# Split projection weights kept in DRAM: stored by the second token block, loaded as two halves by the third and fourth

## The chip, the core and the metric

The kernel runs on one core of one Trainium2 chip. The metric is the device time of one execution in microseconds (us). Engines are named as the profile names them: PE (TensorE matmul), PEld (its weight load), DVE (VectorE), ACT (ScalarE), POOL (GpSimd) and SP (SyncE). SP here does little but issue DMAs; ACT issues a few as well.

## The reference

One decoder block over 2048 tokens of width 1024 in float32. The part that matters here is the combined projection of the mixer:

```python
h = modulate(rms_norm(x, g_pre_mix[l]), shift_m, scale_m)
proj = h @ w_in[l]
q_a, k_a, v_a, q_m, k_m, v_m, o_m, i_m, f_m, g_a, g_m = jnp.split(proj, split_points, axis=-1)
...
y_a = sliding_window_attention(rope(q_a), rope(k_a), v_a, sinks)
h_m = mlstm_chunkwise(q_m, k_m, v_m, i_pre, f_pre)
merged = sigmoid(g_a) * (y_a @ w_branch_attn) + sigmoid(g_m) * (y_m @ w_branch_mlstm)
x = x + gate_m * rms_norm(merged @ w_out, g_post_mix)
```

After this comes a SwiGLU feed-forward with the same kind of norm and gate. `q_a` has 512 columns, `k_a` and `v_a` 128 each, `v_m` 512; the two pre-gates `i_m` and `f_m` have 4 each.

## The kernel before

**Numbers as two halves.** PE multiplies in a format (F32R) that holds fewer bits than float32. So every operand is split in two: `hi` is the value rounded to that format, `lo` the rest. A product is then three matmuls: hi x hi, hi x lo, lo x hi (`mm3`, L283). For weights the split is made by `split` (L255): ACT casts to `whi` (L267, or L264 for q, whose heads are put in pairs, one 512-column slice at a time), DVE subtracts to get `wlo` (L268 or L265).

**Token blocks.** The 2048 tokens go through in four blocks of 512, two to a superblock. Blocks are numbered 0 to 3 in the code; the text calls them one to four. For each block three projections have the tokens on the output's partitions: q (512 columns), kv (264 columns: keys, values, pre-gates) and vm (512 columns, the mLSTM values). Each is a `token_group` (L318): the 1024 input features are eight slices of 128, taken two at a time, which makes four pieces. A piece is 4 token tiles x 2 slices x 3 terms = 24 matmuls into four accumulators (`acc`), evacuated by ACT after the last piece (L778, L805, L829). The first block is written out by hand and takes q and kv in its own way; in it only vm is a `token_group` with loads and splits like the others. The second block takes kv, q, vm; the third q, kv, vm; the fourth kv, q, vm. Every block loads the same columns of `w_in` and splits them again.

**Loads and buffers.** A q or vm load (L298) brings four slices, 1 MB, which serve two pieces; kv comes as one tile for all four pieces (two DMAs, L784 and L785). Loads go into one of two `raw` buffers. A split takes a pair of `split` buffers, of which there are four, so two pairs. A raw buffer is free when its last split has read it; a split pair is free when PE has done the piece.

**What sets the order.** `run2` (L352) goes through all pieces. Before a piece it makes the splits of this piece and the next (`ahead=2`), and issues loads while fewer than two raw tiles are loaded and not yet split. Side work runs in streams that are woven between the matmuls by a count of expected PE time (`now`, with the delays L_...): attention, mLSTM chunks, rotary work on q and k, the next block's norm and transposes. `attend` (L1016) ends the q and k streams and starts attention for the block; `finish` advances the streams with no matmuls of the projection between. The instructions of each engine are then put in a fixed order by the tile scheduler, which runs its own timeline. Each engine, and each DMA-issuing queue, works strictly through that order.

**DRAM in between.** Attention's operands are stored to `at_d` (L771, L798, L816, L818) from tiles called `tx`, of which there are nine, and loaded again (L908, L910); vm goes to `vm_d` (L830). All of these are issued by SP, but for some attention loads and stores by ACT.

Of the kernel before, what the change touches and what calls it, by code (L numbers as in the profile page):

```python
# [10 lines left out]
F32 = mybir.dt.float32  # L11
F32R = mybir.dt.float32r
# [7 lines left out]
P = 128  # L20
S = 2048
D = 1024
KD = D // P
# [31 lines left out]
C_Q, C_K, C_QM, C_KM, C_VM, C_OM, C_IF, C_GA, C_GM = 0, 512, 768, 1280, 1792, 2304, 2816, 2824, 3848  # L55
# [18 lines left out]
def decoder_block(ctx: ExitStack, tc: tile.TileContext, a: dict, out: bass.AP, dbg=None):  # L74
    nc = tc.nc
# [21 lines left out]
    w_in = a["w_in"][0]  # L97
# [6 lines left out]
    wpool = ctx.enter_context(tc.tile_pool(name="wpool", bufs=2))  # L104
# [19 lines left out]
    def tx(shape, dtype=F32):  # L124
        return tpool.tile(shape, dtype, tag="tx", name=nm("tx"), bufs=9)
# [64 lines left out]
    for i in range(HD // 2):  # L190
        f = np.float32(10000.0) ** np.float32(np.float32(-2.0) * np.float32(i) / np.float32(HD))
# [53 lines left out]
    RAWC = KD * 264  # L245
# [6 lines left out]
    def split_tile(name):  # L252
        return wpool.tile([P, 1024], F32R, tag="split", name=nm(name), bufs=4)

    def split(src, shape, pair_heads=False, eng=V):  # L255
        n = int(np.prod(shape))
        hi, lo = split_tile("whi"), split_tile("wlo")
        hv = hi[:, :n].rearrange("p (k c) -> p k c", k=shape[0])
        lv = lo[:, :n].rearrange("p (k c) -> p k c", k=shape[0])
        if pair_heads:  # L260
            for k in range(shape[0]):
                sv = src[:, k, :].rearrange("p (g j d) -> p g j d", g=HKV, d=HD)
                hk, lk = (v[:, k, :].rearrange("p (j g d) -> p g j d", g=HKV, d=HD) for v in (hv, lv))
                A.copy(hk, sv)  # L264
                V.tensor_tensor(lk, sv, hk.bitcast(F32), op=ALU.subtract)  # L265
        else:
            A.copy(hv, src)  # L267
            V.tensor_tensor(lv, src, hv.bitcast(F32), op=ALU.subtract)  # L268
        return hv, lv
# [10 lines left out]
    def piece(raw, view, shape, mms, pair_heads=False):  # L280
        return Part(raw, lambda: split(view(raw.tile), shape, pair_heads), mms)

    def mm3(ps, l, r, first, last):  # L283
        mm(ps, l[0], r[0], first, False)
        mm(ps, l[0], r[1], False, False)
        mm(ps, l[1], r[0], False, last)
# [8 lines left out]
    def raw_rows(w, k0, nk, c0):  # L295
        def load():
            t = raw_tile([nk, 512])
            nc.sync.dma_start(t, w[k0 * P:(k0 + nk) * P, c0:c0 + 512].rearrange("(k p) c -> p k c", p=P))  # L298
            return t
        return Raw(load)  # L300
# [14 lines left out]
            for j in range(2):  # L315
                yield feature_tile(raw, lambda t, j=j: t[:, :, j * P:(j + 1) * P], k, i0 + j, rhs, evac)

    def token_group(srcs, nk, n, lhs, evac, pair_heads=False, stagger=1):  # L318

        acc = []  # L320
        srcs = list(srcs)
        held = []

        def make(si, k0, kc):
            def mms(wt):
                if not acc:
                    acc.extend(acc_tile() for _ in range(NT))
                held.append((wt, k0, kc))
                if len(srcs) - stagger <= si < len(srcs) - 1:
                    return  # L330
                for t in range(NT):
                    for w_, k0_, kc_ in held:
                        for j in range(kc_):
                            kk = k0_ + j
                            mm3(acc[t][:, :n], lhs(kk, t), (w_[0][:, j, :], w_[1][:, j, :]), kk == 0, kk == nk - 1)
                            yield
                    if si == len(srcs) - 1:
                        evac(t, acc[t])
                held.clear()
            return mms  # L340

        for si, (raw, view, k0, kc) in enumerate(srcs):
            yield piece(raw, view, [kc, n], make(si, k0, kc), pair_heads)

    def srcs_rows(w, nk, c0):
        for k0 in range(0, nk, 4):
            kn = min(4, nk - k0)
            raw = raw_rows(w, k0, kn, c0)
            for j in range(0, kn, 2):
                yield raw, (lambda t, j=j: t[:, j:j + 2, :]), k0 + j, 2  # L350
# [350 lines left out]
    def ld(shape, dtype=F32):  # L701
        t = kvp.tile([P, 512], dtype, tag="ld", name=nm("ld"), bufs=4)
        return t.rearrange("p (k c) -> p k c", k=shape[0])
# [24 lines left out]
    om_d = [tc.dram_tile([P, MH, TB], F32, name=f"om_d{i}") for i in range(NBLK)]  # L728
    g_d = [tc.dram_tile([P, 2, KD, TB], F32, name=f"g_d{i}") for i in range(NBLK)]
    y_d = [tc.dram_tile([P, 4, 4, TB], F32, name=f"y_d{i}") for i in range(NBLK)]  # L730
    LOGC = math.log(MD ** -0.5)
    LOG2 = math.log(2.0)

    def superblock(sb):
# [3 lines left out]
        def lhs_h(b):  # L738
            def lhs(kk, t):
                return tuple(p_[:, kk % 4, t * P:(t + 1) * P] for p_ in HC[f"{kk // 4 + 1}{b % 2 + 1}"])  # L740
            return lhs
# [19 lines left out]
        def q_stream(b, t, yz):  # L761
            yield L_ROPE
            y, z = yz
            pt = mix_tile()
            for j in range(GQ):
                transpose(pt[:, j * P:(j + 1) * P], y[:, j * P:(j + 1) * P])
            hi, lo = z.bitcast(F32R), y.bitcast(F32R)
            A.activation(hi, pt, AF.Copy, scale=HD ** -0.5)
            V.scalar_tensor_tensor(lo, pt, HD ** -0.5, hi.bitcast(F32), op0=ALU.mult, op1=ALU.subtract)
            for i, q in enumerate((hi, lo)):  # L770
                nc.sync.dma_start(at_d[b * NT + t][:, i * 512:(i + 1) * 512], q.bitcast(F32))  # L771
# [28 lines left out]
        def evac_kv(b):  # L800
            before = [v_last]

            def evac(t, ps):
                raw = ld([1, 512])[:, 0, :] if b == 0 else tx([P, 392])
                A.copy(raw[:, :264], ps[:, :264])  # L805
                v, dv = raw[:, 128:256], raw[:, 264:392]
                n = b * NT + t
                y = rope(raw, HKV, b, t)
                for i in range(2):
                    A.copy(gt[:, t, 32 * i:32 * i + 4], raw[:, 256 + 4 * i:260 + 4 * i])  # L810
                V.tensor_tensor(dv, v, before[0], op=ALU.subtract)
                before[0] = v
                if t == NT - 1:
                    A.copy(v_last, v)
                    before[0] = v_last
                nc.sync.dma_start(at_d[n][:, AT_V + P:], dv)  # L816
                if n + 1 < S // P:
                    nc.sync.dma_start(at_d[n + 1][:, AT_V:AT_V + P], v)  # L818
                R["qk"].append(spawn(k_stream(n, y)))
            return evac  # L820

        def q_kv(b):
            raw_kv = Raw(load_kv)
            return token_group(srcs_rows(w_in, KD, C_Q), KD, 512, lhs_h(b), evac_q(b), pair_heads=True), token_group([(raw_kv, (lambda r, j=j: r[:, j:j + 2, :]), j, 2) for j in range(0, KD, 2)], KD, 264, lhs_h(b), evac_kv(b))

        def vm(b):
            def evac(t, ps):
                v = tx([P, 512])
                A.copy(v, ps)  # L829
                nc.sync.dma_start(vm_d[b][:, t, :], v)  # L830
            yield from token_group(srcs_rows(w_in, KD, C_VM), KD, 512, lhs_h(b), evac)


        def gates(b):
# [56 lines left out]
            mpv = mp.rearrange("p h (k c) -> p k c h", k=2)  # L891
            V.scalar_tensor_tensor(ex[:, 0], cl[:, :, 0, :], LOGC - LOG2, mpv[:, 1], op0=ALU.add, op1=ALU.add)
            V.tensor_copy(ex[:, 1], cl[:, :, 2, :])
            V.tensor_tensor(ex[:, 2], mpv[:, 0], mpv[:, 1], op=ALU.add)
            A.activation(ex, ex, AF.Exp)
            V.tensor_scalar(cl[:, :, 0, :], cl[:, :, 0, :], LOGC - 2.0 * LOG2, None, op0=ALU.add)
            V.tensor_scalar(mp[:, :, 0:4], mp[:, :, 0:4], -LOG2, None, op0=ALU.add)
# [98 lines left out]
        ready = [0]  # L996
# [358 lines left out]
        for i, (kind, p) in enumerate(pairs):  # L1355
            parts = list(in_pair(kind, p))
            if sb == 0 and i == 4:
                yield lambda: R.update(ada_m=[spawn(ada_stream([(2, "gate")], 6000.0))])
            if i == 0:
                yield from parts[:3]  # L1360
                yield lambda: finish([hps["t"]])
                parts = parts[3:]
            if i + 1 == len(pairs):
# [3 lines left out]
                parts = parts[2:]  # L1367
# [843 lines left out]
```

## Time and profile before

| | us |
|---|---|
| median of 3 runs | 2673.64 (2673.51 to 2677.0) |
| the profiled execution's own time | 2673.95 |
| its span, first to last instruction | 2672.2 |
| PE busy | 2620.8 (98%) |
| DVE busy | 1964.5 (74%) |
| ACT busy | 1304.4 (49%) |
| DMA moved | 511.84 MB, mean 192 GB/s |
| granted clock of PE, mean | 0.995 |

The span is what the profiler sees of the program; the execution's own time is 1.75 us more. The profile gives for each group of instructions its busy time, the mean of one in ns, and the idle time of its engine before it with what ended that time. A row of the waits says who waited for whom: us in total, how often, the longest. In a row of busy times by stretch the columns are the stretch, its length, the busy time of PE, PEld, DVE, ACT and POOL with the instructions' count, the granted clock, the share of the 16 DMA engines that was busy, and what they moved.

In this execution the second block's kv, q and vm pieces run from about 98 to 176 us, the third block's from about 692 to 757, the fourth block's from about 757 to 850.

### The profile page before, as it was taken

The page shows a single profiled execution, that of the slowest core. Times are in us where ns is not written, and L with a number is a line of the kernel's source. Part 1 is how long each engine was busy: PE and PEld are TensorE (multiplying, and loading weights), DVE is VectorE, ACT ScalarE, POOL GpSimd, SP SyncE. Part 2 cuts the span into 40 slices and gives each one's busy share as a digit, 9 for nine tenths or more (in the row PEclk, how much of TensorE's full clock was granted, in tenths as well). Part 3 has the DMA queues.
Part 4 walks back from the last instruction along what each step waited for, and adds up shares of the span by engine and source line. Part 5 has one row for each costly group of instructions (what it writes and reads, how often), then busy time and mean ns, then how long its engine had stood idle before and what let it go on. Part 6 is the DMA issues. An engine that isn't in the chain of part 4 may idle for free.

```text
span 2672.2 us, 36050 instructions
## 1 busy us (share of the span) xinstructions
PE 2620.8 (98%) x12546; PEld 2145.7 (80%) x12546; DVE 1964.5 (74%) x3790; ACT 1304.4 (49%) x2563; POOL 136.3 (5%) x181
## 2 busy tenths in 40 slices
PE   8999999999998999999999999999999999999998
PEld 6877788888876778888878888888778888888886
DVE  6877887768786988875777777775776767676466
ACT  6666544445764654454654443335554333333444
POOL 0000002101100000110000000000000000000000
PEclk9999999999999999999999999999999999999999
DMA  7664455987576645687675555446675323234566
GB/s 269 202 222 138 140 192 182 306 296 256 186 232 197 194 133 165 191 269 294 205 260 173 175 173 177 145 150 215 213 252 180 110 99 105 101 111 138 191 203 221
DMA packets 353062, 511.84 MB, mean 192 GB/s; under 512 B 24544, under 2 KB 213084, under 8 KB 347632
## 3 DMA queue, kind: packets, MB, share of 16 engines
q1 hardware_dynamic: 334664, 493.76, 55.6%
q10 hardware_dynamic: 18216, 15.79, 2.0%
q8 instruction: 99, 1.62, 0.2%
q14 instruction: 83, 0.68, 0.1%
HBM read 357.06 MB, written 144.02 MB: 188 GB/s over the span
## 4 chain that ended last, share of the span: by engine, by line
PE 84%; DVE 6%; DMA 5%; ACT 2%; issue 2%; POOL 0%; SPq 0%; ACTq 0%; DVEq 0%; POOLq 0%
PE acc L212 59%; PE mix L212 22%; PE mix L217 2%; DVE hl L1701 1%; DMA big<-big 1%; PE acc L90 1%; PE mix L90 1%; ACT hl L1700 1%; DMA raw<-as_d 1%; DMA big<-in_x_dram 1%; DMA at<-at_d 1%; DMA raw<-ws_d 1%; DMA at_d<-tx 1%; ACT tm L958 0%; DMA raw<-in_w_ffn_down_dram 0%
## 5 line engine op out<-in xcount | busy, mean ns | idle before, releaser
L212 PE MATMUL acc<-big,hl 128*128 128x512 f32 x3936 | 936.7, 392 | 3.6 <-ACT tx L829 1.5
L212 PEld LDWEIGHTS acc<-big,hl 128*128 128x128 f32 x3936 | 732.2, 188 | 163.5 <-issue 5.5
L1700 ACT CAST hl<-raw 128x512 fp32r<-128x512 f32 x732 | 440.6, 622 | 488.2 <-PE acc L212 219.5
L1701 DVE TENSOR_TENSOR hl<-raw,hl 128x512 fp32r<-128x512 f32 x732 | 496.4, 695 | 198.5 <-ACT hl L1700 195.9
L212 PE MATMUL acc<-whi,big 128*128 128x512 f32 (+1 forms) x1152 | 344.6, 378 | 3.7 <-ACT tx L829 1.6
L212 PE MATMUL mix<-big,hl 128*128 128x512 f32 x1056 | 263.0, 390 | 1.6 <-ACT hl L1700 0.9
L212 PEld LDWEIGHTS acc<-whi,big 128*128 128x128 f32 x1152 | 212.1, 190 | 43.3 <-ACT tx L805 2.4
L212 PE MATMUL acc<-hl,hl 128*128 128x512 f32 x1008 | 237.3, 393 | 5.9 <-DVE hl L1701 3.4
L212 PEld LDWEIGHTS mix<-big,hl 128*128 128x128 f32 x1056 | 197.8, 188 | 44.3 <-DVE hl L1701 1.8
L212 PEld LDWEIGHTS acc<-hl,hl 128*128 128x128 f32 x1008 | 186.9, 188 | 51.6 <-DVE hl L1701 8.8
L212 PE MATMUL acc<-wlo,big 128*128 128x512 f32 (+1 forms) x576 | 217.6, 379 | 3.6 <-DVE wlo L268 3.3
L212 PE MATMUL mix<-hl,hl 128*128 128x512 f32 x792 | 182.9, 391 | 1.2 <-DVE ms L456 0.4
L212 PEld LDWEIGHTS mix<-hl,hl 128*128 128x128 f32 x792 | 147.8, 188 | 35.5 <-DVE hl L1701 3.3
L212 PE MATMUL acc<-big,whi 128*128 128x512 f32 x512 | 157.3, 393 | 0.0
L268 DVE TENSOR_TENSOR wlo<-raw,whi 128x1024 fp32r<-128x1024 f32 (+1 forms) x92 | 106.9, 1163 | 67.2 <-ACT whi L267 61.6
L267 ACT CAST whi<-raw 128x1024 fp32r<-128x1024 f32 (+1 forms) x92 | 91.9, 1000 | 117.3 <-PE acc L212 111.2
L212 PEld LDWEIGHTS acc<-wlo,big 128*128 128x128 f32 x576 | 109.9, 191 | 24.1 <-DVE wlo L268 4.8
L458 POOL TENSOR_TENSOR rs<-ms,halves 128x1 f32<-128x1 f32 (+1 forms) x56 | 41.6, 754 | 1640.2 <-DVE ms L456 1592.3
L212 PE MATMUL mix<-hcT4h,hl 128*128 128x512 f32 x352 | 115.6, 389 | 0.7 <-ACT hl L1700 0.7
L212 PE MATMUL acc<-hcT2h,hl 128*128 128x512 f32 x352 | 115.5, 389 | 0.0
L212 PEld LDWEIGHTS acc<-big,whi 128*128 128x128 f32 x512 | 95.3, 188 | 19.3
L212 PE MATMUL acc<-big,wlo 128*128 128x512 f32 x256 | 97.5, 392 | 0.0
(377 smaller groups left out, 3542.0 us busy)
## 6 DMA issues: line engine op xcount, KB each, us to landing
raw<-in_w_in_dram SPq DMA_DIRECT2D x46, 1024.0 KB, 5.2
as_d<-w SPq DMA_DIRECT2D x154, 256.0 KB, 2.0
raw<-as_d SPq DMA_DIRECT2D x70, 512.0 KB, 3.7
raw<-in_w_ffn_gate_dram SPq DMA_DIRECT2D x22, 1024.0 KB, 5.7
raw<-in_w_ffn_up_dram SPq DMA_DIRECT2D x22, 1024.0 KB, 5.9
raw<-ws_d SPq DMA_DIRECT2D x40, 512.0 KB, 4.5
tx<-in_w_ada_dram SPq DMA_DIRECT2D x64, 256.0 KB, 5.2
g_d<-tx SPq DMA_DIRECT2D x64, 256.0 KB, 2.5
```

Of the source, the lines that this page charges most:

```text
L90: self.last = tc.keep_in_program_order(f(*p, **k)).ins
L212: T.matmul(o, lhsT=lhsT, rhs=rhs, start=start, stop=stop, skip_group_check=resumed)
L217: T.transpose(o, i, ident[:k, :k])
L267: A.copy(hv, src)
L268: V.tensor_tensor(lv, src, hv.bitcast(F32), op=ALU.subtract)
L458: G.tensor_tensor(r[:, :n], ms[:, :n], nhalf[:, :n], op=ALU.pow)
L1700: A.copy(v(hi), src)
L1701: V.tensor_tensor(v(lo), src, v(hi).bitcast(F32), op=ALU.subtract)
```

## The change

The second block, after each split of a q, kv or vm piece, also stores both halves to DRAM arrays `W_D` (24 stores: 512 KB each for q and vm, 264 KB for kv). The third and fourth block no longer load `w_in` for these three and no longer split: they load the halves. Even q and vm pieces go as one 1 MB load of both halves into a raw buffer, odd ones as two 512 KB loads straight into a split pair; kv goes as two loads of 1056 KB, each of two pieces with both halves, into raw buffers. Each such load is a `Raw` of its own, its `Part` has nothing to prepare (`ready` only shapes the views), and the matmuls read the raw tile or split pair directly. So a raw buffer then stays in use up to the piece's last matmul. The matmuls themselves, their count and their operands' values are the same.

```diff
+    def kept_weights(name):
+        n = 528 if name == "kv" else 1024
+        for j0 in range(0, 4, 2):
+            for j in ((j0,) if name == "kv" else (j0, j0 + 1)):
+                def load(j=j):
+                    src = W_D[name]
+                    if name != "kv" and j % 2:
+                        parts = [split_tile(x) for x in ("whi", "wlo")]
+                        for i in range(2):
+                            nc.sync.dma_start(parts[i].bitcast(F32), src[:, j, i, :])
+                        return [parts]
+                    m = 2 if name == "kv" else 1
+                    t = wpool.tile([P, RAWC], F32R, tag="raw", name=nm("raw"))
+                    v = t[:, :m * 2 * n].rearrange("p (m i c) -> p m i c", m=m, i=2)
+                    nc.sync.dma_start(v.bitcast(F32), src[:, j:j + m, :, :])
+                    return [[v[:, q, i, :] for i in range(2)] for q in range(m)]
+                raw = Raw(load)
+                for q in range(2 if name == "kv" else 1):
+                    yield raw, q, 2 * (j + q), 2
...
         for si, (raw, view, k0, kc) in enumerate(srcs):
-            yield piece(raw, view, [kc, n], make(si, k0, kc), pair_heads)
+            if kept:
+                def ready(raw=raw, q=view):
+                    return tuple(v.rearrange("p (k c) -> p k c", k=2) for v in raw.tile[q])
+                yield Part(raw, ready, make(si, k0, kc))
+                continue
+            part = piece(raw, view, [kc, n], make(si, k0, kc), pair_heads)
+            if store:
+                def prep(do=part.prep, si=si, kc=kc):
+                    made = do()
+                    for i, v in enumerate(made):
+                        nc.sync.dma_start(W_D[store][:, si, i, :].rearrange("p (k c) -> p k c", k=kc), v.bitcast(F32))
+                    return made
+                part.prep = prep
+            yield part
...
+    W_D = {x: tc.dram_tile([P, 4, 2, 528 if x == "kv" else 1024], F32, name=f"w_{x}_d") for x in ("q", "kv", "vm")}
...
         def q_kv(b):
+            if b > 1:
+                q = token_group(kept_weights("q"), KD, 512, lhs_h(b), evac_q(b), kept=True)
+            else:
+                q = token_group(srcs_rows(w_in, KD, C_Q), KD, 512, lhs_h(b), evac_q(b), pair_heads=True, store="q" if b else None)
+            if b > 1:
+                return q, token_group(kept_weights("kv"), KD, 264, lhs_h(b), evac_kv(b), kept=True)
             raw_kv = Raw(load_kv)
-            return token_group(...q...), token_group(...kv...)
+            return q, token_group(...kv..., store="kv" if b else None)
...
+            if b > 1:
+                yield from token_group(kept_weights("vm"), KD, 512, lhs_h(b), evac, kept=True)
+            else:
+                yield from token_group(srcs_rows(w_in, KD, C_VM), KD, 512, lhs_h(b), evac, store="vm" if b else None)
```

More of the change, by code (lines that the diff above doesn't have):

```diff
@@ L316, in feature_tiles, with token_group @@
                 yield feature_tile(raw, lambda t, j=j: t[:, :, j * P:(j + 1) * P], k, i0 + j, rhs, evac)
-    def token_group(srcs, nk, n, lhs, evac, pair_heads=False, stagger=1):
+    def kept_weights(name):
[17 more added lines that the diff above has]
+                    yield raw, q, 2 * (j + q), 2
+    def token_group(srcs, nk, n, lhs, evac, pair_heads=False, stagger=1, store=None, kept=False):
         acc = []
@@ L822, in q_kv @@
         def q_kv(b):
+            if b > 1:
[4 more added lines that the diff above has]
+                return q, token_group(kept_weights("kv"), KD, 264, lhs_h(b), evac_kv(b), kept=True)
             raw_kv = Raw(load_kv)
-            return token_group(srcs_rows(w_in, KD, C_Q), KD, 512, lhs_h(b), evac_q(b), pair_heads=True), token_group([(raw_kv, (lambda r, j=j: r[:, j:j + 2, :]), j, 2) for j in range(0, KD, 2)], KD, 264, lhs_h(b), evac_kv(b))
+            return q, token_group([(raw_kv, (lambda r, j=j: r[:, j:j + 2, :]), j, 2) for j in range(0, KD, 2)], KD, 264, lhs_h(b), evac_kv(b), store="kv" if b else None)
         def vm(b):
@@ L830, in evac @@
                 nc.sync.dma_start(vm_d[b][:, t, :], v)
-            yield from token_group(srcs_rows(w_in, KD, C_VM), KD, 512, lhs_h(b), evac)
+            if b > 1:
+                yield from token_group(kept_weights("vm"), KD, 512, lhs_h(b), evac, kept=True)
+            else:
+                yield from token_group(srcs_rows(w_in, KD, C_VM), KD, 512, lhs_h(b), evac, store="vm" if b else None)
         def gates(b):
```

## The prediction

> **What bounds the kernel now.** I read the page first, then who PE waited for, then the busy time by stage.
>
> ```profile
> span 2672.2 us, 36050 instructions
> ...
> PE 2620.8 (98%) x12546; PEld 2145.7 (80%) x12546; DVE 1964.5 (74%) x3790; ACT 1304.4 (49%) x2563; POOL 136.3 (5%) x181
> ```
>
> PE is busy for 2620.8 of 2672.2 us. A change that leaves every matmul in place can win at most the 51 us of PE's idle time, plus what PE loses at a lower clock. So only the stages that the change touches matter. These are the rows of blocks three and four (about 692 to 841 us): who PE waited for from 690 to 842, then busy time by stretch from 716 on (columns: stretch, its length, busy time of PE, PEld, DVE, ACT, POOL, granted clock, DMA share, GB/s).
>
> ```profile
> PE mix L217 <- POOL tm L961: 3.3, 3, 2.8
> PE acc L212 <- DVE wlo L268: 3.3, 3, 2.3
> PE mix L212 <- DMA at<-at_d: 3.1, 1, 3.1
> PE acc L212 <- ACT tx L829: 1.6, 1, 1.6
> ...
> PE mix L217 <- DVE tx L758: 0.5, 1, 0.5
> PE acc L212 <- ACT whi L264: 0.5, 1, 0.5
> ```
>
> ```profile
> 716.00:731.00 15.00, 13.79 (x97) 12.56 (x96) 13.90 (x26) 7.70 (x13) 0.00 (x0) 1.00 0.31 109
> 731.00:755.00 24.00, 21.71 (x126) 18.32 (x125) 21.58 (x56) 17.22 (x35) 0.00 (x0) 1.00 0.80 247
> 755.00:775.00 20.00, 17.97 (x106) 15.35 (x105) 14.20 (x34) 9.56 (x20) 0.00 (x0) 0.93 0.99 358
> 772.40:775.80 3.40, 3.40 (x16) 3.40 (x17) 3.34 (x9) 1.11 (x3) 0.00 (x0) 0.50 0.87 299
> 775.00:800.00 25.00, 24.49 (x150) 21.31 (x150) 23.19 (x75) 17.07 (x64) 4.69 (x4) 0.98 0.47 148
> 820.00:841.00 21.00, 13.49 (x80) 8.16 (x80) 10.78 (x32) 13.25 (x48) 4.69 (x5) 0.76 0.30 90
> ```
>
> PE waits for the splits of weights (wlo L268, whi L264) 3.8 us in all. DVE is 90 to 93% busy from 716 to 755, which is why its splits and its rotary work (L758) come late. The largest loss, 820 to 841, is attention with nothing woven between: 7.5 us idle, and 24% of 21 us lost to the clock.
>
> **What is removed.** Blocks three and four no longer split q, kv and vm. The split groups between 690 and 835 us (busy us, mean ns):
>
> ```profile
> L264 ACT CAST whi<-raw 128x512 fp32r<-128x512 f32 x16 | 9.1, 617 | 2.1 <-PE acc L212 2.1
> L267 ACT CAST whi<-raw 128x1024 fp32r<-128x1024 f32 x6 | 6.3, 1050 | 4.3 <-PE acc L212 4.3
> L267 ACT CAST whi<-raw 128x528 fp32r<-128x528 f32 x8 | 5.1, 637 | 12.0 <-PE acc L212 12.0
> ```
>
> ```profile
> L265 DVE TENSOR_TENSOR wlo<-raw,whi 128x512 fp32r<-128x512 f32 x16 | 11.4, 733 | 8.8 <-ACT whi L264 8.7
> L268 DVE TENSOR_TENSOR wlo<-raw,whi 128x1024 fp32r<-128x1024 f32 x6 | 7.3, 1224 | 3.2 <-ACT whi L267 3.1
> L268 DVE TENSOR_TENSOR wlo<-raw,whi 128x528 fp32r<-128x528 f32 x8 | 5.6, 698 | 1.3 <-ACT whi L267 1.3
> ```
>
> Two of the eight vm pieces lie behind this window; with them ACT sheds 9.1 + 8 x 1.05 + 5.1 = 22.6 us and DVE 11.4 + 8 x 1.22 + 5.6 = 26.8 us. Neither engine sets the end here; the gain is the PE waits that they end. Taken one by one: split waits 3.3 + 0.5 = 3.8 us; rotary wait 0.5; and the half clock from 772.4 to 775.8, which costs 3.4 / 2 = 1.7. That stretch follows a wait for vm's eviction (1.6, ACT tx L829, which I leave: nothing shows that a split held it) and one of the split waits, so I count half of it, 0.8. Gain: 3.8 + 0.5 + 0.8 = **5.1 us**. Bounds: 3.8 if only the direct waits go; 3.8 + 0.5 + 1.6 + 1.7 = 7.6 if all do.
>
> **What is added in block two.** Each of its 12 pieces stores both halves. The weights are 1024 x 512 (q), 1024 x 264 (kv) and 1024 x 512 (vm) floats, 5.28 MB; both halves are 10.55 MB in 24 stores. The stage before:
>
> ```profile
> 98.00:110.00 12.00, 9.92 (x90) 9.17 (x88) 9.21 (x17) 7.31 (x16) 0.00 (x0) 1.00 0.97 333
> 110.00:117.00 7.00, 6.66 (x36) 6.33 (x37) 6.91 (x19) 1.12 (x3) 0.00 (x0) 0.51 0.86 271
> 117.00:130.00 13.00, 11.24 (x67) 9.24 (x66) 8.97 (x39) 11.54 (x48) 2.60 (x3) 1.00 0.07 21
> 130.00:145.00 15.00, 15.00 (x79) 11.43 (x77) 10.01 (x33) 8.25 (x23) 1.73 (x2) 1.00 0.99 295
> 145.00:176.00 31.00, 31.00 (x171) 24.17 (x170) 25.06 (x55) 21.08 (x59) 4.08 (x4) 1.00 0.51 164
> ```
>
> The DMA engines move 333 GB/s at a share of 0.97, so 343 when full. The stores want 10.55 / 0.343 = 31 us of them; idle in these rows are 0.4 + 1.0 + 12.1 + 0.2 + 15.2 = 28.9 us. So the stage becomes full of DMA, and the cover of 117 to 130 is only partly of use, because kv splits before it and the third and fourth q pieces after it:
>
> ```profile
> 112.30 0.41 SPq L298 DMA_DIRECT2D raw<-in_w_in_dram  x1
> ...
> 139.97 0.37 SPq L298 DMA_DIRECT2D raw<-in_w_in_dram  x1
> ```
>
> ```profile
> 117.86 1.14 ACT L264 CAST whi<-raw 128x512 fp32r<-128x512 f32 x2 [3.57 <-PE acc L212]
> ...
> 148.80 1.05 ACT L267 CAST whi<-raw 128x1024 fp32r<-128x1024 f32 x1
> ```
>
> ```profile
> 122.55 0.39 PE L212 MATMUL acc<-wlo,big 128*128 128x512 f32 x1
> ```
>
> q's first load issues at 112.30 behind kv's eight stores (2.16 MB, 6.3 us of full DMA, less the 1.0 us idle): it lands up to 5.3 us later. It now lands in time for the cast at 117.86, and PE's q matmuls begin just before 122.55. With a cast at 117.86 + 5.3 = 123.2 and 1.35 us for the first hi and lo (0.62 + 0.73), PE waits 0 to 2 us; I take 2. The load at 139.97 gets the 2.1 MB of q's last two pieces ahead of it (6.1 us), against a cast at 148.80 that waits for no DMA; attention's next loads share that stretch. I take another 2, bounds 0 to 6. Each store of a lo half waits on SP for its DVE subtract, and rotated keys and queries (at_d) and the next raw load queue behind it; the raw load waits for that same subtract already, so I add nothing for that. A split pair also comes free only when its store has landed: a pair is reused two pieces later, at 5.8 us the soonest (kv, below), and PE's work on those pieces hides the landing; without that cover each landing beyond it delays a split by as much. Block two: **+4 us**, 0 to 8.
>
> **What is added in blocks three and four.** Loads double: +5.28 MB a block, in 14 issues where there were 6. At 343 GB/s that is 15.4 us a block, 31 for both; of which block three's q (2.1 MB, 6 us) comes before 716. The rows from 716 to 800 leave 10.4 + 4.8 + 0.2 + 13.3 = 28.7 us idle for the other 25. The volume fits. What is late next is a buffer: raw tiles used to come free at the split, now at the piece's last matmul. Worst placed is the first piece behind kv, whose buffer is kv's own first half: two kv pieces are left for a load of 1 MB. A piece has 4 token tiles x 2 slices x 3 terms = 24 matmuls; two of them start in 0.24 us here, so two pieces take 5.8 us:
>
> ```profile
> 720.65 0.41 PE L212 MATMUL acc<-whi,big 128*128 128x264 f32 x2
> 720.89 0.28 PE L212 MATMUL acc<-wlo,big 128*128 128x264 f32 x1
> ```
>
> ```profile
> raw<-in_w_in_dram SPq DMA_DIRECT2D x46, 1024.0 KB, 5.2
> ```
>
> The median of 5.2 us fits in 5.8 barely; where DMA is full already (0.99 from 755 to 775) it will be longer. On SP the waiting load stands ahead of at_d stores and the next loads. I take **+1 us**, bounds 0 to 7.5 (three such loads, each 2.5 us late).
>
> **Sum.** The profiled execution took 2673.95 us, 1.75 outside its span and 0.3 over the median of 2673.64. 2673.95 - 5.1 + 4 + 1 = 2673.85; on the median's scale **2673.5**. The smallest case adds 7.6 of gain to no costs, 2666; the largest 3.8 against 8 + 7.5, 2685.
>
> **The clock.** The row 110 to 117 shows 0.51 of the clock behind this wait:
>
> ```profile
> 110.34 0.69 PE L217 MATMUL mix<-ident,tm 68*128 68x68 f32 x4 [2.42 <-DVE tm L868]
> ...
> 752.75 0.51 PE L212 MATMUL acc<-wlo,big 128*128 128x512 f32 x1 [2.27 <-DVE wlo L268]
> ```
>
> 2.42 us of idle time were followed by 7 us at half speed (3.4 us lost), while 2.27 us at 752.75 cost nothing more (the rows to 755 say 1.00). So a new wait over 2 us can cost more than double. The Trainium skill's "TensorE: Matmul & The Clock Gate", Part 1, asks for no PE-idle gaps over about 3.4 us. By that rule no wait that I forecast would lower the clock; the trace disagrees, with 2.42 us that did, so the rivals below go by the row.
>
> **Rivals.** (1) *The lighter DVE carries through, faster.* For it: DVE at 93% and 90% just where PE waits, and a 12.5 us loss at 820 to 841 (7.5 + 0.24 x 21) that begins with a wait for attention's load. Against: that stretch has DVE half idle (10.78 of 21), and its longest waits are POOL and a DMA. With all 7.6 us, a quarter of the 12.5 and 1.5 us for block two: 2673.6 - 7.6 - 3.1 + 1.5 = **2664.4**.
>
> (2) *Block two's stores make DMA the bound, slower.* Place: the loads of 112.30 and 139.97 and attention's loads beside them. For it: 31 us wanted, 28.9 idle. Against: two raw buffers, so that a load has a whole raw tile's matmuls (10.6 us) before it is missed. It decides once a load is more than about 2 us late: waits of 2 and 4 us, each with the 3.4 us of half clock, are 12.8 us; less 5.1: 2673.6 + 7.7 = **2681.3**.
>
> (3) *The split wait is replaced by a load wait, slower.* Kept tiles are freed by PE instead of by the split, and three loads are 2.5 us late, 7.5 us; with 4 for block two and 5.1 gained: 2673.6 + 6.4 = **2680**. Against: DMA is idle at 716 to 731, where block three's load stands.
>
> (4) *The change does not do what it says*: the loads into split tiles wait for the same PE release as the splits did, so that the waits of 3.8 us only change their name. That is the sum without its gain: 2673.5 + 5.1 = **2678.6**.
>
> **How the numbers follow.** Forecast of no change 0.35; (1) 0.33; (2) 0.18; (3) 0.10; (4) 0.04. What a measurement of this kernel can tell from no change is about 0.2%, 5.3 us. (4) lies 5.0 over the median, within that. So faster 0.33, same 0.35 + 0.04 = 0.39, slower 0.18 + 0.10 = 0.28. The forecast's own range is 2669 to 2679. The range for 8 in 10 reaches into the rivals on both sides: 2662 to 2685.
>
> **What would show it.** Right: no casts of L264 and L267 in blocks three and four but those of the branch and output weights, which come later; the rows 716 to 755 with DVE near 70%; split waits gone; DMA share near 1 through most of 92 to 155, and PE waiting there 2 to 6 us more, named DMA or a split behind one. Wrong on the gain's side: the same idle time at 716 to 800 under other names (DMA raw<-w). Wrong on the cost's side: block two's span from 92 to 176 unchanged. What would make the whole wrong is a plan of the instructions that comes out different far from the edit, at 820 to 841 above all, since one such wait is as large as any term here.

## The result and the profile after

| | before | after |
|---|---|---|
| median, us (lowest to highest) | 2673.79 (2672.16 to 2677.0) | 2665.6 (2664.19 to 2666.46) |
| ratio, 95% interval | | 0.9966 [0.9956, 0.9976] |
| profiled execution, its span | 2673.95, 2672.2 | 2664.19, 2662.2 |

The changed kernel is 8.2 us faster. The forecast was no change (2673.5), with a range of 2662 to 2685; what came lies in the range, but has the direction, and nearly the time (2664.4), of rival (1). The head of the page after:

```profile
span 2662.2 us, 36035 instructions
...
PE 2614.5 (98%) x12546; PEld 2142.4 (80%) x12546; DVE 1935.3 (73%) x3758; ACT 1281.4 (48%) x2531; POOL 133.1 (5%) x181
...
DMA packets 352166, 532.95 MB, mean 200 GB/s; under 512 B 23136, under 2 KB 209628, under 8 KB 345200
```

The edit did what it says: 32 instructions fewer on DVE (29.2 us) and on ACT (23.0 us), and 21.1 MB more moved (10.55 stored, 2 x 5.28 loaded). Line numbers after the edit are higher by up to 44: the attention load L910 is now L954, the row maximum's negation L951 is L995.

In blocks three and four, who PE waited for from 690 to 845 us, after:

```profile
PE acc L212 <- DMA raw<-w_kv_d: 3.0, 1, 3.0
PE mix L217 <- POOL tm L1005: 1.9, 1, 1.9
PE mix L212 <- DVE tm L1018: 0.9, 2, 0.5
PE mix L212 <- DMA at<-at_d: 0.9, 1, 0.9
PE mix L212 <- ACT tm L1014: 0.2, 1, 0.2
```

And busy time by stretch, after (the columns are those of the prediction's rows):

```profile
716.00:731.00 15.00, 15.00 (x114) 14.29 (x113) 14.63 (x27) 8.35 (x14) 0.00 (x0) 1.00 0.79 288
731.00:755.00 24.00, 24.00 (x136) 20.74 (x135) 17.09 (x57) 13.18 (x31) 0.00 (x0) 1.00 0.81 252
755.00:775.00 20.00, 16.10 (x102) 13.82 (x102) 15.52 (x39) 8.31 (x18) 0.00 (x0) 0.83 1.00 385
775.00:800.00 25.00, 22.01 (x147) 17.99 (x146) 17.11 (x65) 15.86 (x60) 4.43 (x4) 1.00 0.88 296
...
820.00:841.00 21.00, 21.00 (x119) 15.29 (x117) 12.52 (x32) 7.83 (x23) 2.60 (x3) 1.00 0.50 151
```

The split waits are gone, and the first two rows have PE full. A new wait for block four's kv load (3.0 us) stands in the third row, with the half clock behind it (0.83 of 20 us is 3.4 us lost). The last row shows the largest difference: PE is busy for 21.00 of 21 us at full clock, where it was 13.49 at 0.76.

**Where that row comes from** shows in a chain that begins some 40 us earlier. Block three's attention runs beside block four's projections, in four units of 128 tokens. DVE forms a unit's row maximum and negates it (`nmx`), ACT takes the exponentials, POOL scales, PE multiplies with the values (`mix<-tm,at`), and then the unit's `at` buffer, one of two, is free for the load of the third unit, which ACT issues. These are rows of the timelines of DVE, PE and ACT, before:

```profile
774.18 0.67 DVE L949 TENSOR_REDUCE mx<-tm 128x4 f32<-128x512 f32 x1
...
779.74 0.69 DVE L268 TENSOR_TENSOR wlo<-raw,whi 128x528 fp32r<-128x528 f32 x1
...
782.78 1.27 DVE L265 TENSOR_TENSOR wlo<-raw,whi 128x512 fp32r<-128x512 f32 x2
...
784.65 0.15 DVE L951 TENSOR_SCALAR nmx<-mx 128x8 f32<-128x8 f32 x1
```

```profile
802.15 0.65 PE L212 MATMUL mix<-tm,at 128*64 128x256 f32 x4
```

```profile
807.09 0.34 ACTq L910 DMA_DIRECT2D at<-at_d  x1
816.83 0.34 ACTq L910 DMA_DIRECT2D at<-at_d  x1
```

```profile
823.94 2.93 PE L212 MATMUL mix<-at 64*128 64x256 f32 x24 [3.13 <-DMA at<-at_d]
```

And the same steps after:

```profile
765.78 0.67 DVE L993 TENSOR_REDUCE mx<-tm 128x4 f32<-128x512 f32 x1
...
775.54 0.17 DVE L995 TENSOR_SCALAR nmx<-mx 128x8 f32<-128x8 f32 x1
```

```profile
785.64 0.65 PE L212 MATMUL mix<-tm,at 128*64 128x256 f32 x4 [0.24 <-ACT tm L1014]
...
812.87 1.69 PE L212 MATMUL mix<-at 64*128 64x256 f32 x24
```

```profile
789.12 0.34 ACTq L954 DMA_DIRECT2D at<-at_d  x1
804.50 0.34 ACTq L954 DMA_DIRECT2D at<-at_d  x1
```

Before, weight splits stand on DVE between the parts of the softmax. In the changed kernel the negated row maximum comes 9.1 us sooner, the product with the values 16.5, the third load 18.0 and the last unit's first matmuls 11.1. So the last unit still has projection matmuls woven with it; before, PE's order has none from 819.9 to 841.2.

How much of this the splits in DVE's queue account for, these rows don't show. Between the first maximum and the negation lie 10.5 us before and 9.8 after, and the splits there take only 2.65 us. Most of the lead, 8.4 us, is there at the first maximum already (774.18 and 765.78). Ahead of it, from 756.8 to 763.2, DVE was not full before: it was busy for 1.0 of 6.4 us, and stood idle for 3.08 us of that behind a cast of activations on ACT (L541), which itself waited for its load. After, DVE's order has that work (now L576) behind the first maxima. So another order is part of the lead.

**Block two**, after: who PE waited for from 92 to 176 us, then three stretches.

```profile
PE mix L217 <- POOL tm L1005: 2.2, 1, 2.2
PE mix L217 <- DVE tm L912: 1.6, 1, 1.6
PE acc L212 <- DVE wlo L265: 1.1, 1, 1.1
```

```profile
98.00:110.00 12.00, 10.37 (x90) 9.61 (x90) 11.75 (x24) 6.31 (x15) 0.00 (x0) 0.86 1.02 362
...
117.00:130.00 13.00, 9.55 (x48) 7.24 (x47) 9.44 (x38) 12.65 (x54) 4.28 (x4) 0.87 0.54 195
...
145.00:176.00 31.00, 31.00 (x174) 24.80 (x174) 24.68 (x55) 20.80 (x59) 4.20 (x4) 1.00 0.91 343
```

The DMA share of 145 to 176 went from 0.51 to 0.91, yet PE lost nothing there. The loss is earlier, at 98 to 130, as waits for softmax's division (POOL), the mLSTM's gates (DVE L912) and one split, and as clock.

**The span in stretches.** The marks are PE's first matmul of a kind; each number is from one profiled execution, in us.

| stretch | before | after | stores only | loads only | no stores, single loads |
|---|---|---|---|---|---|
| to block two's kv | 99.3 | 97.0 | 100.1 | 101.7 | 99.2 |
| block two | 89.9 | 92.3 | 91.8 | 89.5 | 89.7 |
| then to block three's kv | 530.1 | 531.0 | 531.7 | 529.0 | 529.0 |
| block three's kv to block four's | 45.9 | 45.9 | 48.3 | 45.8 | 41.6 |
| block four's kv to the output projection | 101.0 | 87.4 | 100.4 | 87.8 | 88.7 |
| then to the feed-forward | 517.2 | 518.5 | 515.1 | 518.9 | 514.5 |
| feed-forward | 1288.7 | 1290.1 | 1291.9 | 1288.5 | 1288.8 |

Block four's stretch gains 13.6 us; block two, the way to block three and all that comes after block four give 2.4 + 0.9 + 1.3 + 1.4 back. The first row differs from kernel to kernel also where nothing ahead of that mark was edited, so I read nothing into it. How far one profile of a stretch can be trusted shows where PE's instructions are in the same order. In block two, the eight kernels of this document that store q, kv and vm have one order, and take 90.7 to 94.4 us; the four that store nothing have another, and take 88.5 to 89.9. The feed-forward has one order in all fourteen kernels, and takes 1288.3 to 1292.4. Blocks three and four together agree better: 133.2 to 133.6 in the three kernels that share the changed kernel's order there. So differences of 1 to 2 us outside blocks three and four say little. Nor is the profiled execution always the middle one: that of "loads alone" took 2662.84 us, against a median of 2658.88.

### The profile page after: what moved, and what is told of

It reads as the page before. It is cut to its first block, busy times and chain, and to the rows that moved or that the text cites. A ratio compares the mean times of both kernels' runs of the same rounds, so it can differ in the third digit from the quotient of the medians.

```text
span 2662.2 us, 36035 instructions
## 1 busy us (share of the span) xinstructions
PE 2614.5 (98%) x12546; PEld 2142.4 (80%) x12546; DVE 1935.3 (73%) x3758; ACT 1281.4 (48%) x2531; POOL 133.1 (5%) x181
## 4 chain that ended last, share of the span: by engine, by line
PE 88%; DVE 5%; DMA 4%; ACT 2%; issue 1%; POOL 0%; ACTq 0%; SPq 0%; DVEq 0%; POOLq 0%
PE acc L212 61%; PE mix L212 23%; PE mix L217 2%; DVE hl L1745 1%; PE acc L90 1%; PE mix L90 1%; ACT hl L1744 1%; DMA raw<-as_d 1%; ACT tm L1002 1%; DMA raw<-ws_d 0%; DMA raw<-w_kv_d 0%; DMA big<-in_x_dram 0%; DMA raw<-in_w_ffn_down_dram 0%; DMA at_d<-tx 0%; DMA raw<-in_w_in_dram 0%
## 5 line engine op out<-in xcount | busy, mean ns | idle before, releaser
L212 PE MATMUL acc<-whi,big 128*128 128x512 f32 (+1 forms) x896 | 279.3, 387 | 0.1
L212 PEld LDWEIGHTS acc<-whi,big 128*128 128x128 f32 x896 | 167.2, 189 | 33.3 <-ACT whi L264 0.4
L212 PE MATMUL acc<-wlo,big 128*128 128x512 f32 (+1 forms) x448 | 173.4, 388 | 1.1 <-DVE wlo L265 1.1
L268 DVE TENSOR_TENSOR wlo<-raw,whi 128x1024 fp32r<-128x1024 f32 (+1 forms) x76 | 91.2, 1200 | 60.9 <-ACT whi L267 55.7
L267 ACT CAST whi<-raw 128x1024 fp32r<-128x1024 f32 (+1 forms) x76 | 78.3, 1031 | 93.9 <-PE acc L212 87.3
L212 PEld LDWEIGHTS acc<-wlo,big 128*128 128x128 f32 x448 | 85.0, 190 | 18.8 <-DVE wlo L265 1.4
```

The costliest lines, as they stand in the source:

```text
L212: T.matmul(o, lhsT=lhsT, rhs=rhs, start=start, stop=stop, skip_group_check=resumed)
```

## The experiments

The theory after the result: **relief**. DVE has less to do, what was queued behind its splits comes sooner, and this reaches a stretch that the named waits don't point to. Against it stand three others: that ACT's relief did it; that another order of the instructions happened to be better, whatever DVE does; and that stores and loads cost nothing. Each expectation below was written before its run. Diffs are cut to the lines that matter and are against the changed kernel, but for the last, which is against the kernel before.

**Stores alone, loads alone.** The first keeps block two's stores and gives blocks three and four back their loads and splits. The second stores nothing and loads the halves from arrays that the kernel writes anyway.

```diff
-            if b > 1:
+            if False:
...
-  store="q" if b else None
+  store="q" if b == 1 else None
```

> Block two stores both halves; blocks three and four load and split as before the change. What the stores cost alone. My prediction put +4 us on them (bounds 0 to 8), and the two traces put block two up to the end of the first superblock at +3.9 us: so 2677.7 us against 2673.8. The rival that the stores hide wholly: 2673.8, and DMA full from 92 to 160 without a wait of PE for it.

```diff
-                    src = W_D[name]
+                    if name == "kv":
+                        src = y_d[0] ...
+                    else:
+                        src = g_d[0 if name == "q" else 1] ...
...
-  store="q" if b else None
+  store="q" if False else None
```

> Blocks three and four load halves of the same size and layout, but from arrays that the program has written anyway (gates and branch outputs of the first blocks), and block two stores nothing. It leaves out the right values of q, kv and vm in blocks three and four; the operations are the same. If the gain of the split's removal and the cost of the stores simply add: 2665.6 - 3.9 = 2661.7 us. The rival that the stores cost nothing: 2665.6.

Stores alone: 2681.61 us, ratio 1.0029 [1.0019, 1.0039], 7.6 us slower. Loads alone: 2658.88, 0.9939 [0.9925, 0.9952], 15 us faster. The two deviations add up to 0.9968; the change has 0.9966. The row of the attention stretch, for stores alone and then for loads alone:

```profile
820.00:841.00 21.00, 13.39 (x98) 9.45 (x97) 10.61 (x32) 13.18 (x48) 4.16 (x4) 0.89 0.43 129
```

```profile
820.00:841.00 21.00, 21.00 (x119) 15.32 (x118) 12.26 (x32) 8.03 (x24) 2.60 (x3) 1.00 0.50 153
```

So the gain comes wholly from blocks three and four, and the stores only cost. From block three's kv to the output projection PE's instructions are in the same order in "loads alone" and in the changed kernel, so the difference of these two isn't one of order there.

**No splits, and no more loading than before.** The loads are of single size, from arrays written anyway, and each serves as both halves; block two stores nothing. The lines of the loads are left out below.

```diff
-                    return tuple(v.rearrange("p (k c) -> p k c", k=2) for v in raw.tile[q])
+                    return (raw.tile[:, 2 * q:2 * q + 2, :],) * 2
```

> Neither stores nor splits nor doubled loads: blocks three and four load 1 MB for two pieces, as before the change, from arrays written anyway, and PE uses the loaded tile as both halves. It leaves out the lo half and the right values; matmuls and all other operations are the same. The gain of the relief alone. If doubling the loads costs the 1 us that I put on it, 1 us under the run that loads both halves without stores, about 2660.7; if the wait for the kv load in block four (3.05 us and 6.8 us at half clock in the changed kernel's trace) is what doubling costs, about 2655.

2654.97 us, 0.9927 [0.9914, 0.9939]. Against "loads alone" the doubled loads cost 3.9 us; the intervals of the two overlap, so this is a size and not a proof. Its profile has 41.6 us for block three's stretch, 4.3 under the kernel before. Taking the splits away is worth 19 us by the medians when nothing is paid for it.

**The work put back, by engine.** The halves are loaded as in the changed kernel, and an operation of the split's size is done in place on them: by both engines, by DVE alone, by ACT alone. The values don't change.

```diff
-                    return tuple(v.rearrange("p (k c) -> p k c", k=2) for v in raw.tile[q])
+                    hi, lo = (v.rearrange("p (k c) -> p k c", k=2) for v in raw.tile[q])
+                    for k in range(2) if pair_heads else (slice(0, 2),):
+                        A.copy(hi[:, k, :], hi[:, k, :].bitcast(F32))
+                        V.tensor_tensor(lo[:, k, :], lo[:, k, :].bitcast(F32), lo[:, k, :].bitcast(F32), op=ALU.max)
+                    return hi, lo
```

> The changed kernel, but each loaded piece of blocks three and four gets an ACT cast of its hi half and a DVE operation on its lo half in place, of the sizes that the split had (q by slice), which leave the values as they are. If the gain comes from the work taken off ACT and DVE (22.6 and 26.8 us), it goes: 2673.8 + 3.9 or so, about 2678 us, with DVE at 90% from 716 to 755 again. The rival that it comes from another order of the instructions or from the loads going straight to their place: it stays near 2666.

The next two keep one of the two lines, `V.tensor_tensor` and `A.copy`.

> The changed kernel with only the DVE work put back in blocks three and four (in place, on the lo halves), not ACT's. If DVE, at 90 to 93% busy from 716 to 755 before, is the engine whose relief counts: as with both put back, about 2674 us. If it is ACT, on which attention's exponentials stand behind the casts: about 2666.

> The changed kernel with only the ACT casts put back (in place, on the hi halves). With DVE's work put back alone the gain was gone (2677 us). If DVE is the one engine that counts: about 2666. If either engine's work is enough to make attention late in block four: about 2674, as with both put back.

| | median | ratio |
|---|---|---|
| both | 2674.12 | 0.9993 [0.9985, 1.0002] |
| DVE's alone | 2677.33 | 1.0009 [1.0, 1.0018] |
| ACT's alone | 2665.47 | 0.9959 [0.9947, 0.9972] |

Against the kernel before, the gain is gone with DVE's work back; with ACT's back it is all there. But these kernels also pay the stores, and against stores alone (2681.61) not all of the 16 us is gone: 4.3 are left with DVE's work back, and 7.5 with both engines'. So the work put back takes away 12 and 8.5 of the 16 us. What gives the rest was not isolated. Nor can work alone explain that the kernel with more of it put back is the faster one (2674.12 against 2677.33): some 3 us here are the order, which differs between these kernels in blocks three and four, or chance.

The kernel with DVE's work, the stretch in which the chain of attention runs, two waits of PE and one of ACT in it, and the third attention load:

```profile
775.00:800.00 25.00, 18.51 (x116) 14.28 (x117) 23.16 (x70) 16.05 (x60) 2.22 (x2) 0.76 0.89 323
```

```profile
788.60 1.12 PE L217 MATMUL mix<-ident,tm 128*128 128x128 f32 x4 [2.57 <-POOL tm L1008]
...
795.88 2.08 PE L212 MATMUL acc<-raw,big 128*128 128x512 f32 x4 [2.62 <-DMA raw<-w_q_d]
```

```profile
797.31 0.40 ACT L1005 ACTIVATE tm<-tm,nmx 128x128 f32<-128x128 f32 x1 [3.29 <-DVE nmx L998]
...
800.88 0.34 ACTq L957 DMA_DIRECT2D at<-at_d  x1
```

And the kernel with ACT's work, the same stretch and load:

```profile
775.00:800.00 25.00, 20.20 (x123) 14.88 (x123) 17.23 (x64) 21.38 (x74) 4.52 (x4) 0.93 0.91 336
```

```profile
788.76 0.34 ACTq L957 DMA_DIRECT2D at<-at_d  x1
```

DVE is busy for 23.16 of 25 us in the first, as in the kernel before (23.19), and ACT's exponentials wait 3.29 us for the row maximum. In the second DVE is busy for 17.23 and ACT for 21.38; the load is issued at 788.76, as in the changed kernel (789.12). So ACT being busier than before at that place (17.07) doesn't delay the load; but PE is busy for 20.20 us at 0.93 of the clock there, less than in the changed kernel (22.01 at 1.00).

The loss with DVE's work back is not that of the kernel before, come back at its place. At 820 to 841 PE is busy for 19.91 of 21 us at full clock. The loss stands at 785 to 800 instead, where PE is busy for 8.51 of 15 us at 0.61 of the clock, and begins with a wait for softmax's division on POOL (2.57); later in it comes one for a load of q's halves (2.62), which is no work of DVE's.

**One block alone.** Only block three, or only block four, takes the halves; block two stores in both.

```diff
-            if b > 1:
+            if b == 2:
```

> Block two stores; only block three loads the halves, block four loads and splits as before the change. In the traces of the changed kernel and of the runs so far the stretch from block four's first kv matmul to the end of the front part is 101 us before, 87 to 89 with the work gone, 98 with it put back; block three's stretch hardly differs. If the gain sits in block four, this is the stores' 7.6 us alone: about 2681 us. If each block has half of the gain: about 2673.

> Block two stores; only block four loads the halves, block three loads and splits as before. If the gain sits in block four: 2674 + 7.6 - 13.6 = 2668 us, or a little less, since 5.3 MB fewer are loaded. If each block has half of it: about 2673.

Block three alone: 2673.35, 0.9996 [0.9987, 1.0005]. Block four alone: 2680.44, 1.0022 [1.0013, 1.0031]. Block three alone came where half of the gain in each block was to put it, but block four alone missed both of its sizes (2668 and 2673). By the medians, block four's splits alone are worth 1.2 us against stores alone (2681.61), block three's 8.3, and both together 16. The two are not a sum. The stretches of one profile each say it otherwise: blocks three and four together take 148.7 us with stores alone, 142.8 with block three alone, 141.3 with block four alone and 133.3 after. Block four alone then takes 3.8 us more on the way to the feed-forward (518.9 against 515.1). In block four alone PE still waits for block three's splits, here from 690 to 845:

```profile
PE acc L212 <- DVE wlo L268: 4.4, 2, 2.9
PE mix L217 <- DVE tm L987: 2.6, 1, 2.6
```

A plain reading is that block three's splits delay what attention needs and block four's splits delay its softmax, so that either alone keeps the chain late; the next table agrees with it in part, but no run isolates it.

**How late the third attention load is, and how long block four takes.** Both are counted from block four's first kv matmul, in us, from one profile each; the load is the first that ACT issues there.

| kernel | third load issued | block four's stretch |
|---|---|---|
| before | 41.8 | 101.0 |
| stores alone | 40.2 | 100.4 |
| block three alone | 35.5 | 97.6 |
| both engines' work back | 34.7 | 98.3 |
| DVE's work back | 32.9 | 98.1 |
| block four alone | 31.0 | 92.5 |
| kv split as before | 28.5 | 87.2 |
| kv split as before, arrays placed last | 27.0 | 87.3 |
| no splits, single loads | 26.6 | 88.7 |
| ACT's work back | 24.9 | 94.4 |
| arrays placed last | 23.0 | 87.8 |
| after | 23.0 | 87.4 |
| subtracts on POOL | 22.9 | 87.7 |
| loads alone | 22.9 | 87.8 |

With a load up to 29 us the stretch takes 87 to 89, and over 32 us 98 to 101; at 31.0 it is 92.5. The two go together; that the load sets the time isn't shown by that, and in the kernel with DVE's work back the loss came elsewhere. ACT's work is the exception: an early load, yet 94.4, of which 4.9 us are made up for in block three (41.0).

**Less of the change, and another place.** One kernel leaves kv to be split as before and keeps q and vm; one places the arrays behind all others in DRAM, to see if their addresses matter to the feed-forward; one does both.

```diff
-    W_D = {x: ... for x in ("q", "kv", "vm")}
+    W_D = {x: ... for x in ("q", "vm")}
```

> The changed kernel with kv left as before the change in all blocks (split each time, not stored); q and vm are stored and loaded. It drops 2.16 MB of stores at 93 to 115 us, where DMA is full, and block four's kv load, for which PE waited 3.05 us with 6.8 us of half clock. If those cost what the trace shows and kv's own splits hide: 2665.6 - 3 - 3 - 1.5 = about 2658 us. If the relief of kv's splits is what lets block four's attention run early: about 2670.

> The changed kernel with the three DRAM arrays of the weights placed behind all others, so that the feed-forward's arrays keep the addresses that they had before the change; PE's instructions are the same. In the profiles with stores the feed-forward, whose instructions are the same in all, takes 1288 to 1292 us, in those without the arrays 1288.5 to 1288.8. If the moved addresses cost that: about 2 us under the changed kernel, 2663.5. If it is chance between executions: 2665.6.

> kv left as before the change in all blocks, q and vm stored and loaded, and the arrays placed last. It should be the best of both: 2662.8 with the arrays where they were, so 2661 if the addresses cost 2 us, 2662.8 if not.

2662.81, 0.9954 [0.9942, 0.9967]; 2664.17, 0.9954 [0.994, 0.9967]; 2664.31, 0.9955 [0.9942, 0.9967]. None can be told from the changed kernel, and neither size that was expected of leaving out kv (2658 or 2670) came. Without the kv arrays the 3.0 us load wait is gone, but PE waits for kv's splits again (2.1 us) and block three's stretch grows to 49.9. That the address of the arrays matters is not shown.

**The subtract on another engine.** The kernel before, with only the subtracts of blocks three and four moved from DVE to POOL: nothing is stored or loaded twice.

```diff
-                V.tensor_tensor(lk, sv, hk.bitcast(F32), op=ALU.subtract)
+                eng.tensor_tensor(lk, sv, hk.bitcast(F32), op=ALU.subtract)
...
+    def token_group(srcs, nk, n, lhs, evac, pair_heads=False, stagger=1, eng=V):
...
+ eng=G if b > 1 else V
```

> The kernel before the change (no stores, no kept halves), with the subtract of the q, kv and vm splits of blocks three and four moved from DVE to POOL, which is 5% busy. POOL takes 1.13 to 1.39 us for 128x512, so 2.3 to 2.8 for a q or vm piece whose matmuls take 5.3. If DVE's relief is the gain, and POOL keeps up, it has that gain without the stores' 7.6 us and the doubled loads' 4: like the run without stores and splits at best, 2655, and under 2664 in any case. If splits that come later on POOL hold up PE, or attention's division on POOL (L961) queues behind them: 2668 or more. If the gain came with the loads of halves and not with DVE's relief: 2674.

2672.36, 0.9991 [0.9982, 1.0]: hardly anything, and a miss against the "under 2664 in any case" of relief; what came is the rival that splits on POOL hold up PE. Block four's stretch does fall to 87.7, as relief has it, with nothing stored and no halves loaded; but block three's grows from 45.9 to 54.2. The timelines of POOL, DVE and PE in it:

```profile
734.75 2.38 POOL L268 TENSOR_TENSOR wlo<-raw,whi 128x1024 fp32r<-128x1024 f32 x1 [7.05 <-ACT whi L267]
741.22 8.82 POOL L268 TENSOR_TENSOR wlo<-raw,whi 128x1024 fp32r<-128x1024 f32 x1 [4.09 <-ACT whi L267]
```

```profile
735.80 1.88 DVE L527 TENSOR_TENSOR big<-big,big 128x512 f32<-128x512 f32 x1
...
747.96 2.19 DVE L837 TENSOR_TENSOR gt<-gt,b_if 128x16 f32<-128x16 f32 x2
```

```profile
750.09 0.79 PE L212 MATMUL acc<-wlo,big 128*128 128x512 f32 x1 [4.99 <-POOL wlo L268]
```

One subtract took 2.38 us, and beside it a DVE operation that takes 0.68 at other times took 1.88. The next subtract of that size took 8.82, while DVE ran nearly nothing but two-input operations, without a gap, from 740 to 748; PE waited 4.99 us for it. At its end DVE stood in turn: two 128x16 additions took 2.19 us (0.26 in the kernel before). The Trainium skill's "SBUF — State Buffer", section "SBUF: two separate sides", says that DVE operations with two SBUF inputs and GpSimd share a port pair as an exclusive lock, and that the other engine blocks fully. These rows agree with it.

## Where the prediction was right and where wrong, step by step

**What is removed: this step failed.** It took the gain to be the PE waits that carry a split's name, 5.1 us, at most 7.6. The work of that step was right (DVE shed 29.2 us, ACT 23.0, forecast 26.8 and 22.6), and so was "neither engine sets the end here" for ACT. For DVE it was wrong. Taken by itself the removal is worth 19 us, and putting DVE's operations back takes away 12 of the 16 us that it is worth where the stores are paid. The part that the waits don't name is that attention comes late: before, the row maximum is 9 us later than after, the third attention load 18 us, and at the end of the block 12.5 us of PE time are lost under the names of POOL and a DMA. How much of that is DVE's queue and how much another order stays open.

**Rival (1)** named the place, and was given a quarter of those 12.5 us; all of it went. The argument against it ("that stretch has DVE half idle") looked for the cause in the stretch of the loss. As far as the work put back shows, the cause lies at 716 to 800, where DVE was busy for 72.9 of 84 us and attention's softmax stood between splits. The prediction had that row too (23.19 of 25 at 775 to 800) and drew nothing from it.

**What is added in block two: 4 us, bounds 0 to 8.** The whole kernel pays 7.6 [5.1, 10.4], near the upper bound. Block two itself pays 2.4 in the changed kernel's profile and 1.9 with stores alone; the mean of the eight kernels with these stores is 3.3 over that of the four with none (92.7 and 89.4). So at its place the term was about right. What it pays there isn't the two late loads: the waits are for softmax, the mLSTM's gates and one split, 4.9 us against 4.2, and the clock loses 1.7 us more. That the pair of a split would come free in time ("PE's work on those pieces hides the landing") was wrong for kv. ACT in block two, after:

```profile
108.29 0.63 ACT L267 CAST whi<-raw 128x528 fp32r<-128x528 f32 x1 [2.05 <-DMA w_kv_d<-whi]
```

And q's first load, then issued at 114.94 instead of 112.30, though block two begins 2.3 us sooner there:

```profile
114.57 0.32 SPq L374 DMA_DIRECT2D w_kv_d<-wlo  x1
114.94 0.43 SPq L298 DMA_DIRECT2D raw<-in_w_in_dram  x1
```

The rest of the 7.6 us must be in stretches without a store. With stores alone the profile has 2.4 us more in block three, where PE's order is that of the kernel before, and block four alone, with the same order there, has 2.9 more. The profile of stores alone also has 1.6 us more before block three's kv and 3.2 in the feed-forward (1291.9 against 1288.7), but the ten kernels that store take 1288.3 to 1292.4 there, and the four that don't 1288.5 to 1289.5, so one profile can't place it. What the stores do there stays open; the kernel with the arrays placed last didn't settle it.

**What is added in blocks three and four: 1 us, bounds 0 to 7.5.** About 4 us, a size and not a proof as said above. The place was right, "where DMA is full already (0.99 from 755 to 775)". The load that came late was kv's own first, not the piece behind kv, and no buffer held it at its issue: SP issued it right behind an attention load (754.09, 0.33 us), and PE had it 11.7 us later. Buffers did hold other loads of halves: SP waited 19.4 us for PE before six of them from 690 to 800, and PE paid nothing for these. The first kv load of block four, and PE's wait for it:

```profile
754.48 0.43 SPq L333 DMA_DIRECT2D raw<-w_kv_d  x1
```

```profile
766.17 4.30 PE L212 MATMUL acc<-raw,big 128*128 128x264 f32 x18 [3.05 <-DMA raw<-w_kv_d]
```

It was sized by one such wait of 1 us, without the clock; the wait was 3.05 and the clock cost another 3.4. "A new wait over 2 us can cost more than double" stood two paragraphs further on and wasn't applied to this term.

**Rivals (2) to (4).** (2) priced two late loads in block two, with their half clock, at 12.8 us; PE has no wait for a load there, and the block pays 2 to 3. (3) held for one load. (4) is refuted: the waits for splits are gone, and the one load wait stands at another place.

**What would show it.** DVE at 716 to 755 was to be near 70%; it is 31.7 of 39 us, 81%, since it did other work there sooner. "A plan of the instructions that comes out different far from the edit, at 820 to 841 above all" was named as what could make the whole wrong. It did come out different. How much of the gain is a new order and how much the same order done sooner can't be told apart by these runs: each kernel that gives DVE its work back also gets another order.

The costs were too small by 3.6 and 3 us and the gain by 14; that the time came out within the stated range is luck, since these partly cancel.

## What to carry to other kernels

Work taken off an engine that is over 90% busy can be worth more than the waits that carry that work's name, as here: follow what else stands in its queue (here softmax) to the loads and buffers behind it, and to the next stretch where PE has nothing woven. Price the costs with the clock: a wait of 3 us cost 6.5. And test gain and payment apart, stores alone, loads alone, and the work put back on one engine at a time, each against the kernel that pays the same costs; here 19 us of gain were hidden behind some 11 us of costs.

## What the runs showed of the hardware

A subtract of 128x1024 on POOL took 2.38 us where it went first and 8.82 behind DVE's two-input operations; on DVE it takes 1.22. After a wait of 3.05 us PE lost 3.4 us to the clock. The Trainium skill's "TensorE: Matmul & The Clock Gate", Part 1, which the prediction weighed, puts the limit at gaps of about 3.4 us; as with the 2.42 us of the kernel before, the trace has it lower. DMA moved 385 GB/s over 755 to 775 after, at a share of 1.00; the prediction reckoned with 343 for a full one, by which its 31 us for the stores would be 27; with the stores, over 98 to 110, it moved 362 at 1.02.
